# Sums of squares stored as rows, the last results of a projection stored at once, and four more weight blocks split ahead, in a two-attention encoder layer

## The chip, the cores and the metric

The kernel runs on one core of a Trainium2 chip. A core has TensorE (PE; its weight loads are listed as PEld), VectorE (DVE), ScalarE (ACT), GpSimd (POOL) and SyncE (SP), which here only issues DMAs; 16 DMA engines move data between HBM and the core's own memory. The metric is the device time of one execution in microseconds: the median of three runs, and beside it one profiled execution, whose trace gives every instruction's start and length.

## The reference

One encoder layer is applied to two independent requests of 2048 tokens each (a "prompt" and a "sample") with the same weights, in float32:

```
h    = RMSNorm(x)                                  # x: 2048 x 1024
proj = h @ w_in    -> q_a 512 | k_a 128 | v_a 128 | g_a 512 | q_b 512 | k_b 512 | v_b 512 | g_b 512
o_a  = windowed GQA (8 query heads, 2 key heads, +-128 tokens, QK-norm, partial rotary, sink) * SiLU(g_a)
o_b  = 2-D neighbourhood attention (8 heads, grid 32 x 64, QK-norm, position bias)            * SiLU(g_b)
x    = x + concat(o_a, o_b) @ w_out                # 1024 x 1024
y    = x + (p @ w_ple) * sigmoid(x @ w_ple_gate)   # p: 2048 x 256
```

## The kernel before, in words

**Precision by splitting.** TensorE multiplies in a reduced float32 format, so each operand is split into a high part (a rounded copy) and a low part (the rest), and each product is made of three: high x high, high x low, low x high. A weight block is 128 x 512; split it is 128 x 2 x 512 (512 KB). Splitting takes one ScalarE instruction for the high part and one VectorE instruction for the low one.

**Fillers and units.** The work is written as two streams that are woven together. *Fillers* are the projections of one tile of 128 tokens: `proj_a(f)` for f = 0 to 31 (attention A, 16 tiles per request), then `proj_b(f)` for f = 32 to 95 (attention B, whose heads are done in two halves of four: f = 32 to 63, then 64 to 95). *Units* are the attention of one tile. A table of fractions (PLAN_A, PLAN_B) says at which point of a filler each step of a unit is issued; attention lags its projection by 2 tiles in A and by 6 in B. The order on TensorE is fixed by hand (every matmul is pinned behind the one before). For the other engines and for the DMA queue a planner orders the instructions at build time by the order in which they are written and by its own estimate of when each is ready; `P(...)` pins an instruction behind the one written just before it on the same engine, and `behind(...)` pins one behind the last matmul.

**Weights of attention B split ahead.** While A's 28 fillers f = 2 to 29 run, `presplit` takes one weight block each: it loads the raw block (256 KB) into a staging buffer of tag `raw`, splits it in the middle of the filler, and at the next filler stores both parts to HBM (`parts_d`, 512 KB). It handles 28 of the 32 blocks of attention B; the other four (second half, `wb`, odd j) are copied as they are to HBM (`plain_d`). When the stream reaches a half, `load_w` loads its 16 blocks: `wa` while the last two tiles' second projections run, `wb` after them. A whole block in parts is one load; a plain one is loaded raw and its split is put on a list (`jobs`) that the fillers work off.

**Sums for the last stage.** `combine` forms sums and differences of the quarters of `w_out` and `w_ple_gate` in 8 rounds of six steps: load 1 MB into the same `raw` buffer, four subtractions or additions on POOL, store 1 MB. Each `proj_b` from f = 32 on takes one step, every eighth takes two; all is done at f = 75. From then on `presplit` handles 16 more blocks (of `w_ple` and `w_out`), one per tile.

**The norm.** In A each tile's mean square (`ms`, one number per token, so one column of 128 x 1) is made from a second, token-major load of x (`stn<-x_n`, two of 256 KB per tile) by two ScalarE squares. B's tiles hold the tokens in another order, so every `proj_a` stores its column to HBM (`ms_d`, L601), and at the end of each request `regroup` lists 16 gathers (`ms_b<-ms_d`, L639) that bring the numbers back in B's order, two per filler.

**The last layers' results.** When the fillers run out, the stream turns to `ple_ahead(n)`, n = 0 to 7, which makes p @ w_ple for 512 tokens in 8 blocks of six matmuls; each block goes from PSUM (tag `pj`, three banks) by a ScalarE copy to a buffer `ev` and by DMA to HBM (`ple_d`). The store is written one step late: `store_ple(1)` issues the store of the block before. The first five n run beside the last attention units; the last three are the tail: TensorE has nothing else to do, `ev` rotates through five buffers of tag `s`, and between them the first loads of the last stage are written (`load_raw`, 1 MB each; `load_x`, 256 KB each; `load_q`, four of 256 KB).

**The last stage** multiplies by `w_out` and `w_ple_gate` with seven block products in place of eight (`product`, accumulators `acca` and `accc`). Its first product puts its four column blocks into PSUM tags `ms`, `ms`, `pj`, `pj`.

Of the kernel before, what the change touches and what calls it, by code (L numbers as in the profile page):

```python
# [11 lines left out]
F32 = mybir.dt.float32  # L12
# [5 lines left out]
SEQ = 2048  # L18
DM = 1024
NT = SEQ // 128  # L20
# [80 lines left out]
def emit(ctx, tc, io):  # L101
# [73 lines left out]
    def w_block(half, tag, j):  # L175

        if half == "p":
            return io["w_ple"][128 * j:128 * j + 128, 512 * tag:512 * tag + 512]
        if half == "o":
            h, c = int(tag[2]) - 1, int(tag[1]) - 1  # L180
            return io["w_out"][512 * h + 128 * j:512 * h + 128 * j + 128, 512 * c:512 * c + 512]
        c0 = 1280 + 1024 * half + (512 if tag == "wb" else 0)
        return io["w_in"][128 * j:128 * j + 128, c0:c0 + 512]

    def load_w(half, tag):

        ws = []
        hold[0], step[0] = HOLD[tag], 4
        for j in range(KT):
            w = main.tile([128, 2, 512], F32R, tag=f"{tag}{j}", name=f"{tag}{j}", bufs=1)  # L190
            if (half, tag, j) in parts_d:
                nc.sync.dma_start(w.bitcast(F32), parts_d[half, tag, j])
            else:
                raw = w[:, 1].bitcast(F32)
                nc.sync.dma_start(raw, plain_d[half, tag, j])
                jobs.append((f"{tag}{j}", partial(split_w, w, raw, nw[:, j:j + 1], P)))
            ws.append(w)
        return ws

# [2 lines left out]
    def presplit(load):  # L202

        if load:
            if due:
                key, t, slot = due.pop()
                nc.sync.dma_start(parts_d[key], t[:, 0:2].bitcast(F32))
            if to_split:
                if not pre:
                    pre.extend([ap.tile([128, 4, 512], F32R, tag="raw", name="pre", bufs=1), 0])  # L210
                pre[1] += 1
                due.append((to_split.pop(0), pre[0], 2 + pre[1] % 2))
                key, t, slot = due[0]
                nc.sync.dma_start(t[:, slot].bitcast(F32), w_block(*key))
        elif due:
            key, t, slot = due[0]
            raw, sc = t[:, slot].bitcast(F32), nw[:, key[2]:key[2] + 1]
            if key[0] in ("p", "o"):
                behind(nc.scalar.copy(t[:, 0], raw))
                behind(nc.vector.tensor_tensor(out=t[:, 1], in0=raw, in1=t[:, 0].bitcast(F32), op=ALU.subtract))  # L220
            else:
                behind(nc.scalar.activation(t[:, 0], raw, AF.Copy, scale=sc))
                behind(nc.vector.scalar_tensor_tensor(out=t[:, 1], in0=raw, scalar=sc, in1=t[:, 0].bitcast(F32),
                                                      op0=ALU.mult, op1=ALU.subtract))
# [192 lines left out]
    for i in range(2):  # L417
        split(1, i)
    blocks = [(half, tag, j) for half in range(2) for tag in ("wa", "wb") for j in range(KT)]
    parts_d = {(half, tag, j): dram.tile([128, 2, 512], F32, tag=f"sp_{half}{tag}{j}", name=f"sp_{half}{tag}{j}")  # L420
               for half, tag, j in blocks if half == 0 or tag == "wa" or j % 2 == 0}
    for half, tag, j in [("p", m, j) for m in range(2) for j in range(2)] + \
            [("o", name, j) for name in ("a11", "a12", "a22") for j in range(4)]:
        parts_d[half, tag, j] = dram.tile([128, 2, 512], F32, tag=f"sp_{half}{tag}{j}", name=f"sp_{half}{tag}{j}")
    to_split = list(parts_d)
    plain_d = {}
    for key in blocks:
        if key not in parts_d:
            plain_d[key] = dram.tile([128, 512], F32, tag="pl_%d%s%d" % key, name="pl_%d%s%d" % key)
            copies.append((plain_d[key], w_block(*key)))  # L430
    sums = [dram.tile([4, 128, 4, 512], F32, tag=f"sums{i}", name=f"sums{i}") for i in range(2)]
    w_gate_c = copied(io["w_gate"], DM, 1024)
    snk = ap.tile([128, 2, 8], F32, tag="snk", name="snk")
# [58 lines left out]
    def proj_a(f):  # L492
# [105 lines left out]
        else:  # L598
            gate()
        held[f] = q, gs, y  # L600
        P(nc.sync.dma_start(ms_d[128 * f:128 * f + 128].rearrange("(p c) -> p c", c=1), ms))  # L601
        if t == NT - 1:
            regroup(s)
        else:
            regroup_next()
# [155 lines left out]
    def proj_b(f):  # L761
        half, st = divmod(f - 2 * NT, 2 * NT)
        s, j = divmod(st, NT)
        b, cb = divmod(j, 4)
        if f < 2 * NT + 8:
            regroup_next()
        if not ks_b:
            ks_b.extend(big([128, 32, 2, 64], F32R, f"ks_b{e}") for e in range(2))
        w_qk, w_vg = w_b[half]
        xr = xt.pop(f)  # L770
        pk = ptile([128, 512], "pj", "pqk")
        for i, c in enumerate(project(pk, xr, lambda k, b: ready("wa", k, w_qk)[:, b, :], 215)):
            at = i + 24 if f in last else i
            if i == PD and f == 2 * NT + 9:
                stats_b(1)
            if at in HX:
                split(f + 1, HX[at])
            if i == PA and combined and (to_split or due):
                presplit(True)
            yield c  # L780
        sq = ap.tile([128, 512], F32, tag="sq", name="sqb", bufs=2)
        nc.scalar.activation(sq, pk, AF.Square)
        ssq = ap.tile([128, 8], F32, tag="ssq", name="ssqb", bufs=3)
        nc.vector.tensor_reduce(out=ssq, in_=sq.rearrange("p (h d) -> p h d", d=HD), op=ALU.add, axis=AX.X)
        vr = ap.tile([128, 8], F32, tag="vr", name="vrb", bufs=2)
        y = ap.tile([128, 8], F32, tag="y", name="yb", bufs=4)
        nc.vector.tensor_scalar(out=vr, in0=ssq, scalar1=1.0 / HD, scalar2=ep_b[:, st:st + 1],  # L787
                                op0=ALU.mult, op1=ALU.add)
        rsqrt(vr, y, 8)
        qg = ap.tile([128, 2, 4, HD], F32, tag="qg", name="qg", bufs=6)  # L790
        kt = ap.tile([128, 4, HD], F32, tag="kt", name="kb", bufs=2)
        def normed():

            for dst, c in ((kt, 4), (qg[:, 0], 0)):
                behind(nc.vector.tensor_tensor(out=dst, in0=pk[:, 64 * c:64 * c + 256].rearrange("p (h d) -> p h d", d=HD),
                                               in1=y[:, c:c + 4].unsqueeze(2).broadcast_to([128, 4, HD]), op=ALU.mult))
        yield 0, False
        pv = ptile([128, 512], "pj", "pvg")
        for i, c in enumerate(project(pv, xr, lambda k, b: ready("wb", k, w_vg)[:, b, :], 215)):
            if i + 24 in HX and f not in last:  # L800
                split(f + 1, HX[i + 24])
            if i == (PR if f not in last else 1):
                normed()
            if i == PA + 16:
                presplit(False)
            yield c
            if i == (KB if f not in last else 10):
                if f < 2 * NT + 2:
                    pending.append((kt, b, cb))
                else:  # L810
                    keys_b(kt, b, cb)
        v = ap.tile([128, 4, 2, HD], F32R, tag="sq", name="vb", bufs=2)
        vp = pv[:, 0:256].rearrange("p (h d) -> p h d", d=HD)
        nc.scalar.activation(v[:, :, 0, :], vp, AF.Copy, scale=rs_b[:, st:st + 1])
        nc.vector.scalar_tensor_tensor(out=v[:, :, 1, :], in0=vp, scalar=rs_b[:, st:st + 1],
                                       in1=v[:, :, 0, :].bitcast(F32), op0=ALU.mult, op1=ALU.subtract)
        for w, (c0, ncol) in COL_WIN.items():
            lo, hi = max(c0, 16 * cb), min(c0 + ncol, 16 * cb + 16)
            if lo < hi:
                nc.sync.dma_start(v_d[half, s, w][8 * b:8 * b + 8, lo - c0:hi - c0].rearrange("r c h a d -> c r (h a d)"),  # L820
                                  v[8 * (lo - 16 * cb):8 * (hi - 16 * cb)].bitcast(F32).rearrange("p h a d -> p (h a d)"))
        gs = qg[:, 1].rearrange("p h d -> p (h d)")
        nc.scalar.activation(gs, pv[:, 256:512], AF.Tanh, scale=hr_b[:, st:st + 1])
        nc.vector.scalar_tensor_tensor(out=gs, in0=gs, scalar=1.0, in1=pv[:, 256:512], op0=ALU.add, op1=ALU.mult)
        held[f] = qg[:, 0], gs
        for _ in range(2 if f % 8 == 4 else 1):
            if next(combining, 0) == 0:
                combined.append(f)
        yield 0, False
# [152 lines left out]
    def store_ple(n):  # L982

        for dst, ev in made[:n]:
            nc.sync.dma_start(dst, ev)
        del made[:n]

    def ple_ahead(n, tail=False):

        load_p(n + 1)  # L990
        for m in range(KT):
# [14 lines left out]
                ev = ap.tile([128, TW], F32, tag=("ev", "sq")[m // 2 % 2], name="ev", bufs=3 - m // 2 % 2)  # L1006
            P(nc.scalar.copy(ev, ps))
            store_ple(1)
            made.append((ple_d[n][:, m], ev))

    qs = {}

# [98 lines left out]
                keys_b(*p)  # L1111
            owed = 16
    drain(stream)
    store_ple(1)


    ab_stack.close()
    with tc.tile_pool(name="c", bufs=1, reuse_waits="tile") as op:
# [183 lines left out]
            piece(0, k)  # L1302
        load_q(0, "s2")
        drain(rest)
        store_ple(1)
        for _ in range(4):
            load_x()
        for name in ("s1", "s3", "s4"):
# [95 lines left out]
```

## Time and profile before

| | |
|---|---|
| median of 3 runs | 2491.75 us (2488.02 to 2493.52) |
| the profiled execution | 2489.69 us, its span 2487.9 us |
| fillers of A with A's attention | 0 to about 720 us |
| turn to B's first half, then fillers 34 to 37 alone | about 720 to 812 us |
| first half of B, second half of B | about 812 to 1191, 1245 to 1740 us, the turn between them |
| p @ w_ple beside the last units, then alone | about 1740 to 1831 to 1871 us |
| last stage | 1871 us to the end |
| DMA | 438.87 MB, mean 176 GB/s |

How to read it: a row of a wait names who stood idle and what came last before it went on; a row of the chain gives a start, a length and the work; a row of SyncE's queue gives an issue of a DMA and not its landing. "PEclk" or the column before the DMA share is the clock that TensorE was granted, 1.00 being full speed.

### The profile page before, as it was taken

The page shows a single profiled execution, that of the slowest core. Times are in us where ns is not written, and L with a number is a line of the kernel's source. Part 1 is how long each engine was busy: PE and PEld are TensorE (multiplying, and loading weights), DVE is VectorE, ACT ScalarE, POOL GpSimd, SP SyncE. Part 2 cuts the span into 40 slices and gives each one's busy share as a digit, 9 for nine tenths or more (in the row PEclk, how much of TensorE's full clock was granted, in tenths as well). Part 3 has the DMA queues.
Part 4 walks back from the last instruction along what each step waited for, and adds up shares of the span by engine and source line. Part 5 has one row for each costly group of instructions (what it writes and reads, how often), then busy time and mean ns, then how long its engine had stood idle before and what let it go on. Part 6 is the DMA issues. An engine that isn't in the chain of part 4 may idle for free.

```text
span 2487.9 us, 40537 instructions
## 1 busy us (share of the span) xinstructions
PE 2459.3 (99%) x13048; PEld 2078.0 (84%) x13048; DVE 1702.9 (68%) x4210; ACT 1413.9 (57%) x3405; POOL 863.4 (35%) x1365
## 2 busy tenths in 40 slices
PE   9999999999999999999999999999999999999999
PEld 7888888888878888888788888888777888888887
DVE  6777777777765666666666666666536655687776
ACT  6777776777664665565656566666653222344443
POOL 5555555555444544544444444443100000000000
PEclk9999999999999999999999999999999999999999
DMA  7655554455374566555855566667876445756765
GB/s 204 143 111 96 98 88 102 96 92 98 82 195 137 167 190 183 169 167 184 288 171 184 177 205 210 199 198 239 295 255 233 161 169 175 267 171 219 243 227 169
DMA packets 247140, 438.87 MB, mean 176 GB/s; under 512 B 32400, under 2 KB 86800, under 8 KB 241680
## 3 DMA queue, kind: packets, MB, share of 16 engines
q1 hardware_dynamic: 246640, 436.27, 59.6%
q8 instruction: 104, 1.70, 0.3%
q14 instruction: 108, 0.88, 0.1%
q10 hardware_dynamic: 288, 0.01, 0.0%
HBM read 308.24 MB, written 133.19 MB: 177 GB/s over the span
## 4 chain that ended last, share of the span: by engine, by line
PE 91%; DMA 4%; DVE 3%; ACT 1%; issue 1%; POOL 0%; SPq 0%; ACTq 0%; DVEq 0%; POOLq 0%
PE pqk L255 14%; PE acca L1226 14%; PE pvg L255 14%; PE accc L1226 10%; PE pg L255 6%; PE pq L255 5%; PE scb L255 4%; PE ptb L258 3%; PE pob L255 3%; PE pple L255 3%; PE pk L255 3%; PE po L255 3%; PE sc L255 3%; PE pt L258 2%; DMA stn<-x_n 1%; DMA vw<-v_d 1%
## 5 line engine op out<-in xcount | busy, mean ns | idle before, releaser
L287 ACT ACTIVATE s<-s,nm 128x320 f32<-128x320 f32 (+6 forms) x512 | 294.4, 576 | 314.9 <-DVE nm L282 193.9
L255 PE MATMUL pvg<-wb,xr 128*128 128x512 f32 x1536 | 462.6, 408 | 1.3 <-DMA wb<-sp_0wb 0.6
L255 PE MATMUL pqk<-wa,xr 128*128 128x512 f32 x1536 | 442.9, 410 | 0.0
L255 PEld LDWEIGHTS pqk<-wa,xr 128*128 128x128 f32 x1536 | 266.1, 189 | 36.9
L255 PEld LDWEIGHTS pvg<-wb,xr 128*128 128x128 f32 x1536 | 266.7, 189 | 34.2 <-DMA wb<-sp_0wb 2.2
L1208 ACT CAST opd<-raw 128x512 fp32r<-128x512 f32 x224 | 131.5, 618 | 273.3 <-PE acca L1226 115.2
L356 POOL TENSOR_TENSOR xr<-stx,xr 128x512 fp32r<-128x512 f32 x188 | 241.6, 1295 | 106.3 <-ACT xr L355 84.0
L1209 DVE TENSOR_TENSOR opd<-raw,opd 128x512 fp32r<-128x512 f32 x224 | 146.4, 685 | 151.7 <-ACT opd L1208 151.7
L255 PE MATMUL pg<-wb,xr 128*128 128x512 f32 x768 | 233.5, 410 | 1.8 <-DVE vv L518 1.0
L255 PE MATMUL pq<-wa,xr 128*128 128x512 f32 x768 | 219.4, 400 | 0.0
L271 DVE CUSTOM_DVE_ANT_0 s<-scb,bias 128x288 f32<-128x288 f32 (+3 forms) x256 | 142.0, 555 | 104.6 <-PE scb L255 104.5
L137 POOL TENSOR_TENSOR yb<-vrb,power 128x8 f32<-128x8 f32 x64 | 106.5, 1664 | 236.1 <-DVE vrb L787 222.6
L1226 PE MATMUL accc<-opd,wb 128*128 128x512 f32 x768 | 176.7, 389 | 0.0
L1226 PE MATMUL acca<-opd,wa 128*128 128x512 f32 x768 | 176.6, 391 | 0.0
L1226 PE MATMUL acca<-opd,s 128*128 128x512 f32 x768 | 175.4, 389 | 0.0
L1226 PEld LDWEIGHTS acca<-opd,wa 128*128 128x128 f32 x768 | 145.1, 189 | 30.3
L1226 PEld LDWEIGHTS accc<-opd,wb 128*128 128x128 f32 x768 | 144.2, 188 | 29.9
L1226 PEld LDWEIGHTS acca<-opd,s 128*128 128x128 f32 x768 | 144.2, 188 | 29.9
L918 DVE TENSOR_TENSOR otb<-pob,otb 64x512 f32<-64x512 f32 x128 | 88.1, 689 | 112.8 <-ACT otb L917 111.2
L255 PEld LDWEIGHTS pob<-p_t,vw 128*128 128x128 f32 (+2 forms) x832 | 133.0, 189 | 27.6 <-DVE p_t L899 5.0
L255 PEld LDWEIGHTS pq<-wa,xr 128*128 128x128 f32 x768 | 135.1, 189 | 17.3
L715 DVE TENSOR_TENSOR pr<-pt,pr 128x512 fp32r<-128x512 f32 (+2 forms) x248 | 135.5, 549 | 16.5 <-ACT pr L713 13.2
(167 smaller groups left out, 5177.0 us busy)
## 6 DMA issues: line engine op xcount, KB each, us to landing
stx<-x_b SPq DMA_DIRECT2D x128, 256.0 KB
vw<-v_d SPq DMA_DIRECT2D x112, 256.0 KB
stx<-x_a SPq DMA_DIRECT2D x64, 256.0 KB
stn<-x_n SPq DMA_DIRECT2D x64, 256.0 KB
v_d<-vb SPq DMA_DIRECT2D x64, 256.0 KB
ple_d<-ev SPq DMA_DIRECT2D x64, 256.0 KB
xres<-x_r SPq DMA_DIRECT2D x64, 256.0 KB
x_d<-r SPq DMA_DIRECT2D x64, 256.0 KB
```

Source lines behind the costliest of these rows:

```text
L137: nc.gpsimd.tensor_tensor(out=y, in0=v, in1=power.broadcast_to([128, n]), op=ALU.pow)
L255: pinned(nc.tensor.matmul(out, lhsT, rhs, start=start, stop=stop))
L258: pinned(nc.tensor.transpose(out, in_, eye))
L271: nc.vector.tensor_tensor_reduce(out=s, in0=ps[:, :n], in1=bias, scale=1.0, scalar=-3.0e38, op0=ALU.add, op1=ALU.max, accum_out=sm["mx"][: ...
L287: ex = nc.scalar.activation(ss[i], ss[i], AF.Exp, bias=nm[:, i:i + 1], accum_out=den[:, i:i + 1])
L356: low.tensor_tensor(out=lo, in0=raw, in1=hi.bitcast(F32), op=ALU.subtract)
L715: nc.vector.tensor_tensor(out=pr[r, 1, to], in0=pt[r, c], in1=pr[r, 0, to].bitcast(F32), op=ALU.subtract)
L918: nc.vector.tensor_tensor(out=ot[a:a + 64], in0=pq[a:a + 64], in1=ot[a:a + 64], op=ALU.add)
L1208: P(nc.scalar.copy(hi, v))
L1209: P(nc.vector.tensor_tensor(out=lo, in0=v, in1=hi.bitcast(F32), op=ALU.subtract))
L1226: pinned(nc.tensor.matmul(ps, w[k][:, a, c:c + 128], o[:, b], start=i in (0, 1, 4) and k == 0 and j == 0, stop=k == 3 and j == 2, skip_gro ...
```

## The change

1. `proj_a` no longer stores its column of mean squares. At the last tile of each request the 16 columns are transposed by TensorE into a PSUM buffer of tag `ms`, copied by ScalarE into a buffer of tag `sq`, and stored as 16 rows of 128 numbers (512 B) in one DMA.
2. In the tail, `ple_ahead` writes each store right behind its own copy; the step that was owed at the end is dropped in both places.
3. All 32 blocks of attention B are split ahead. The list of raw copies in HBM and the split at the load are gone. The 28 fillers of A still take 28 blocks; the last four (second half, `wb`, j = 4 to 7) are taken by f = 34 to 37, stored by f = 38, and the staging buffer is then given free.
4. `combine` starts at f = 39 and takes two steps at every third tile, one at the others; it is done at f = 75.

```diff
@@ load_w
-            if (half, tag, j) in parts_d:
-                nc.sync.dma_start(w.bitcast(F32), parts_d[half, tag, j])
-            else:
-                raw = w[:, 1].bitcast(F32)
-                nc.sync.dma_start(raw, plain_d[half, tag, j])
-                jobs.append((f"{tag}{j}", partial(split_w, w, raw, nw[:, j:j + 1], P)))
+            nc.sync.dma_start(w.bitcast(F32), parts_d[half, tag, j])
@@ presplit
-            if to_split:
+            if to_split and (to_split[0][0] in (0, 1) or combined):
                 if not pre:
                     pre.extend([ap.tile([128, 4, 512], F32R, tag="raw", name="pre", bufs=1), 0])
...
                 nc.sync.dma_start(t[:, slot].bitcast(F32), w_block(*key))
+            else:
+                pre.clear()
@@ emit
-               for half, tag, j in blocks if half == 0 or tag == "wa" or j % 2 == 0}
+               for half, tag, j in blocks }
...
-    plain_d = {}
-    for key in blocks:
-        if key not in parts_d:
-            plain_d[key] = dram.tile([128, 512], F32, tag="pl_%d%s%d" % key, name="pl_%d%s%d" % key)
-            copies.append((plain_d[key], w_block(*key)))
@@ proj_a
-        P(nc.sync.dma_start(ms_d[128 * f:128 * f + 128].rearrange("(p c) -> p c", c=1), ms))
         if t == NT - 1:
+            ps = ptile([128, 512], "ms", "pms")
+            tr(ps[:NT, :128], ms_a[:, NT * s:NT * s + NT])
+            row = ap.tile([128, 512], F32, tag="sq", name="row", bufs=2)
+            P(nc.scalar.copy(row[:NT, :128], ps[:NT, :128]))
+            P(nc.sync.dma_start(ms_d[s * SEQ:(s + 1) * SEQ].rearrange("(t p) -> t p", p=128), row[:NT, :128]))
             regroup(s)
@@ proj_b
-            if i == PA and combined and (to_split or due):
+            if i == PA and f >= 2 * NT + 2 and (to_split or due):
                 presplit(True)
...
-        for _ in range(2 if f % 8 == 4 else 1):
+        for _ in range(0 if f < 2 * NT + 7 else 2 if f % 3 == 0 else 1):
             if next(combining, 0) == 0:
                 combined.append(f)
@@ ple_ahead
             store_ple(1)
-            made.append((ple_d[n][:, m], ev))
+            if tail:
+                nc.sync.dma_start(ple_d[n][:, m], ev)
+            else:
+                made.append((ple_d[n][:, m], ev))
@@ after drain(stream), and after drain(rest)
-    store_ple(1)
```

More of the change, by code (lines that the diff above doesn't have):

```diff
@@ L1304, in emit @@
         drain(rest)
-        store_ple(1)
         for _ in range(4):
```

## The prediction

> **What bounds the kernel now.** I read the page first (its engine totals and the shares of the chain that ended last), then the trace cut into stages, then the list of TensorE's own waits, and last the chain and SyncE's queue around the longest of them.
>
> ```profile
> span 2487.9 us, 40537 instructions
> PE 2459.3 (99%) x13048; PEld 2078.0 (84%) x13048; DVE 1702.9 (68%) x4210; ACT 1413.9 (57%) x3405; POOL 863.4 (35%) x1365
> PE 91%; DMA 4%; DVE 3%; ACT 1%; issue 1%; POOL 0%; SPq 0%; ACTq 0%; DVEq 0%; POOLq 0%
> ```
>
> TensorE is busy 99% of the span and makes 91% of the chain. No matmul is added or taken away here (two tiny transposes apart), so a gain can only come out of the places where TensorE stands still or runs slowly. The stages (the columns are time, then busy time of PE, PEld, DVE, ACT, POOL, the granted clock, DMA share, GB/s) say where those are:
>
> ```profile
> 0.00:720.00 720.00, 709.09 (x4247) 620.22 (x4248) 546.21 (x1679) 505.06 (x1396) 382.31 (x793) 1.00 0.54 114
> 1191.00:1245.00 54.00, 52.55 (x281) 42.81 (x280) 36.61 (x88) 34.16 (x77) 23.15 (x26) 1.00 0.86 294
> 1245.00:1740.00 495.00, 495.00 (x2700) 416.29 (x2698) 334.16 (x849) 306.17 (x723) 217.51 (x252) 1.00 0.63 197
> 1740.00:1831.00 91.00, 87.77 (x480) 73.11 (x479) 51.04 (x130) 64.28 (x151) 13.88 (x28) 0.98 0.79 270
> 1831.00:1871.50 40.50, 34.82 (x149) 28.19 (x148) 7.71 (x13) 17.44 (x32) 0.73 (x1) 0.94 0.90 306
> 1871.50:2488.00 616.50, 610.57 (x2688) 504.92 (x2687) 424.49 (x678) 211.55 (x377) 0.00 (x0) 1.00 0.61 201
> ```
>
> And the waits of TensorE itself (who it waited for: us in total, times, longest):
>
> ```profile
> PE pple L255 <- ACT ev L1007: 5.7, 1, 5.7
> PE pt L258 <- DVE ot L742: 5.4, 2, 4.9
> PE pob L255 <- DMA vw<-v_d: 2.6, 4, 1.5
> PE pg L255 <- DVE vv L518: 1.0, 1, 1.0
> PE pktb L258 <- DVE kb L795: 0.7, 1, 0.7
> PE pvg L255 <- ACT wb L151: 0.4, 1, 0.4
> PE pvg L255 <- DVE wb L152: 0.3, 1, 0.3
> ```
>
> Two single waits, of 5.7 and 4.9 us, are most of it. Each part of the change touches one group of these waits, so I take them in that order.
>
> **Part 1, the sums of squares.** The wait of 4.9 us lies at 679.35. The chain there (start, length, what), SyncE's queue, and ScalarE's wait in it:
>
> ```profile
> 666.34 9.18 DMA stn<-x_n
> 675.60 0.69 ACT stn L369 x2
> 678.89 0.42 DVE ot L742
> 679.35 1.12 PE pt L258 x4
> ```
>
> ```profile
> 662.75 0.80 SPq L601 DMA_DIRECT2D ms_d<-ms_a  x1
> 666.34 1.58 SPq L338 DMA_DIRECT2D stn<-x_n  x2
> ```
>
> ```profile
> ACT stn L369 <- DMA stn<-x_n: 4.9, 1, 4.9
> ```
>
> ScalarE's square stands in its queue in front of the attention's output copies, and it waits for a 256 KB load that needs 9.18 us. Why so long? An undisturbed load of the same kind takes a third of that, and during the slow one the DMA engines are half busy but move almost nothing (second fence, first row; its other two rows are used below):
>
> ```profile
> 35.04 2.83 DMA stn<-x_n
> ```
>
> ```profile
> 667.00:674.00 7.00, 7.00 (x43) 6.00 (x42) 2.84 (x13) 2.39 (x9) 4.58 (x13) 1.00 0.50 20
> 679.40:682.00 2.60, 2.60 (x13) 2.60 (x14) 2.48 (x6) 1.67 (x4) 0.00 (x0) 0.50 0.18 53
> 1868.60:1873.00 4.40, 4.40 (x11) 3.43 (x12) 0.00 (x0) 1.37 (x4) 0.00 (x0) 0.50 1.03 393
> ```
>
> A share of 0.50 at 20 GB/s means packets that sit and wait. What went out just ahead is the store of one column of `ms_a`, 128 separate words of 4 bytes side by side in one 512-byte stretch of HBM. My reading is that those 128 small writes hold up the load behind them. The Trainium skill (DMA: Bandwidth & Descriptors, Specifications) states that a transfer under 512 B is done as a read-modify-write; the row of 20 GB/s agrees, though the page does not say that others are held up.
>
> The change takes all 32 of these stores out and puts two in, each of 16 rows of 512 B. At 666.34 the load should then need about 2.8 us and be there near 669.2 (the second of the pair, 1.2 us later, near 670.5), while ScalarE is busy with exponentials until about 675.60 - 4.9 = 670.7. So 4.9 us of idle time go. After the wait TensorE runs 2.6 us at a granted clock of 0.50, which costs 2.6 / 2 = 1.3 us. In the stretch from 1191 to 1245, whose waits are 0.7 us at most, the clock is 1.00 throughout, so I let the half clock go with the wait. **Gain 6.2 us.** The Trainium skill (TensorE: Matmul & The Clock Gate, Part 1) puts the half rate down to an idle window of about 3.4 us; the trace agrees, since the 0.50 stands behind waits of 4.9 and 5.7 us, and by that rule a wait that is only halved would already give back the same 1.3 us. What is late next is nothing that I can see: VectorE itself waited for ScalarE there. The other 30 column stores cost TensorE nothing that the list of waits shows, since the loads behind them had time; 32 issues of up to 0.8 us leave SyncE's queue, where nothing was late because of them. The 32 gathers of the same words (`ms_b`) stay.
>
> Added at tiles 15 and 31: one transpose, one PSUM buffer of tag `ms`, one copy, one 8 KB store.
>
> ```profile
> L258 PE MATMUL pt<-ident,s 128*128 128x128 f32 x616 | 98.4, 273 | 6.1 <-DVE ot L742 5.4 <-DVE den L295 0.7
> L741 DVE TENSOR_TENSOR ot<-po,ot 64x256 f32<-64x256 f32 x128 | 54.0, 422 | 89.9 <-ACT ot L738 89.0
> ```
>
> A transpose is at most 0.27 us. It must wait for one of two `ms` buffers, which the output copies give back; VectorE's part of that sat idle 89.9 / 128 = 0.7 us before each, two of them per buffer. Bounds: 0.1 us (pipelined) to 0.27 + 1.4 + 0.8 = 2.5 us each. I take 0.25 each, near the lower end, since the plan issues the buffer's last copies ahead of it (`fin` at 0.45 of a half unit of 720 / 64 = 11.2 us, the new transpose near 0.59, so 1.5 us). **Cost 0.5 us.** The queue behind the store (weight loads for the next stage) waits for one copy of about 0.6 us.
>
> **Part 2, results stored at once.** SyncE's queue and the chain at the longest wait:
>
> ```profile
> 1853.29 3.30 SPq L1245 DMA_DIRECT2D xres<-x_r  x4
> 1856.64 0.43 SPq L1158 DMA_DIRECT2D raw<-oa_d  x1
> 1857.12 0.50 SPq L1160 DMA_DIRECT2D raw<-ob_d  x1
> 1857.72 2.05 SPq L985 DMA_DIRECT2D ple_d<-ev  x3
> ```
>
> ```profile
> 1857.72 10.09 DMA ple_d<-ev
> 1868.55 2.93 PE pple L255 x6
> ```
>
> The 24 last copies rotate through five buffers of tag `s`. Counted from 0, copy 20 reuses the buffer of copy 15. The store of copy 15 is written one step late, so it stands behind four loads of 256 KB and two of 1 MB, 3 MB in all, and lands after 10.09 us. TensorE's last six products need the PSUM bank that copy 20 frees. With the store written at its own copy, `load_x` and both `load_raw` are pinned behind it; it goes out in their place, about 1854, with nothing large ahead, and lands some 3 us later. Copy 20 is due near 1861: the wait began at 1868.55 - 5.7 = 1862.9, and its products ended two blocks of six earlier, 2.7 us before that. Copy 21 now waits, for the store of copy 16, which stays behind the 3 MB. But the last products need only copies up to 20, and the first two column blocks of the next product use `ms` banks. Only the third uses a bank that copy 21 frees. It begins 24 products later. At the last stage's rate (610.57 / 2688 = 0.227 us) TensorE would end the last six near 1864.2 and those 24 near 1869.7. The stores behind the 3 MB landed at 1857.72 + 10.09 = 1867.8, so the margin is 1.9 us. So the 5.7 us go, and with them the half clock of the quoted 4.4 us, 2.2 us. **Gain 7.9 us.** Moving the store puts the six loads behind it some 0.7 us later, which the margin takes. If it doesn't, the third block waits for what is missing.
>
> **Part 3, the last four blocks.** At the turn to the second half, four of eight `wb` blocks are loaded raw and split on the spot, and the splits sit in ScalarE's and VectorE's queues until the load is there:
>
> ```profile
> 1225.82 7.17 DMA wb<-pl_1wb
> 1233.01 0.73 ACT wb L151
> 1233.76 0.75 DVE wb L152
> ```
>
> They account for 0.4 + 0.3 us of TensorE's waits and, as the chain runs on from them through VectorE to `kb`, for the 0.7 us of `pktb`. **Gain 1.4 us.** Against it stand 4 x 256 KB = 1 MB more to load. At the stage's 294 GB/s that is 3.5 us of queue, the upper bound of a cost.
>
> ```profile
> 1223.30 0.58 SPq L623 DMA_DIRECT2D sums<-raw  x1
> ```
>
> But this 1 MB store now leaves the stage. Counting steps (two at every third tile from 39), stores fall at tiles 60 and 65, none at 63. Bytes balance, so I take 0. The four raw copies in HBM go too, and the eight copies of `w_gate` behind them move up by two tiles, to tiles 2 to 5; no wait of TensorE above is laid to them, 0. The same four splits return at tiles 34 to 37, where projections run alone, each about 0.73 + 0.75 us in two engines that are not the bound. Their 4 x 768 KB there meet a combining that no longer runs before tile 39.
>
> The combining keeps its 32 operations on POOL and ends at tile 75 as before. New is that at tiles 39, 48, 57 and 66 the first operation follows its own load at once, so POOL may stand until 1 MB is there.
>
> ```profile
> L137 POOL TENSOR_TENSOR yb<-vrb,power 128x8 f32<-128x8 f32 x55 | 91.6, 1665 | 218.0 <-DVE vrb L787 204.5 <-DMA stx<-x_b 9.0 <-DMA raw<-w_gate 4.4
> ```
>
> POOL idles 218.0 / 55 = 4.0 us ahead of each of these anyway. Bounds for the four: nothing, if the load takes the 2.83 us of an undisturbed one; 10.09 - 4.0 = 6.1 us each, if it is as slow as the slowest quoted. I take 0: DMA is not full outside the turns. Behind a standing POOL are the gate products and `o_tb`, for which VectorE waits.
>
> **Sum**, against the profiled execution's own 2489.69 us (span 2487.9): -6.2 + 0.5 - 7.9 - 1.4 = -15.0, so 2474.7. The median of the runs shown stands 2.1 us above that execution; from 2491.75 it is **2476.8**.
>
> **Rivals.**
>
> *The slow loads are slow by themselves* (reading `x_n`, not the stores). For: the first stage, the only one that reads `x_n`, moves 114 GB/s at a DMA share of 0.54, the second half of B 197 at 0.63, so slow packets are common in it. Against: the 2.83 us at 35.04, the same load with no such store just ahead. Then only parts 2 and 3 count: -7.9 - 1.4 + 0.5 = -8.8, 2483.0.
>
> *The tail's wait comes back elsewhere*, on copy 21, on the 1 MB loads, or because copy 15 itself comes late and the pinned loads wait with it. For: DMA runs at 0.90 there and the margin is 1.9 us. Against: the loads' total stays the same. Then -6.2 - 1.4 + 0.5 = -7.1, 2484.7.
>
> *Slower*: POOL stands behind the sums' loads at the four tiles, VectorE waits for `o_tb` and TensorE for VectorE. At 6.1 us each plus the half clock after it (1.3 to 2.2, say 1.7) that is 31 us, less 15 gained: 2508. It decides from 15 / 4 = 3.8 us per place. Against it: between 1245 and 1740 TensorE waits for nobody.
>
> **How the numbers follow.** 0.2% (5 us) is about what a measurement of this kernel can tell from no change. The sum above 0.60; slow loads by themselves 0.10; tail not mended 0.10; both failing, or a reshuffled order eating the gain, 0.09 (about 2490); slower 0.11. The first three are faster by over 0.2%: 0.80. The likeliest case alone: 2471 to 2481, its low end taking in the 1.0 us of `vv`, 2.5 us of `vw` and the spread of the runs, its high end 2 us per transpose. The range reaches to the two partial cases and a little beyond: 2470 to 2487.
>
> **What would show it.** Part 1: no `ms_d` issue but two, `stn` landing in about 3 us throughout, no wait of `pt` near 679, no half clock there. Part 2: the store ahead of `xres`, `pple` waiting for nothing, `acca` starting some 14 us earlier than 1871.5 (6.2 - 0.5 + 1.4, then 5.7 and half of 2.9 at the half clock). Part 3: no `wb` split. Wrong would be: slow `stn` with `ms_d` gone; a new wait at `acca`'s third block; POOL idle over 5 us on `raw`.

## The result, and the profile after

| | before | after |
|---|---|---|
| median of 6 runs | 2492.64 us (2488.02 to 2497.40) | 2473.18 us (2471.06 to 2475.98) |
| the profiled execution | 2489.69 us, span 2487.9 | 2471.06 us, span 2469.3 |

The ratio is 0.9922, 95% interval 0.9908 to 0.9935: faster by 19.5 us between the medians and by 18.6 us between the two profiled executions, where 15.0 was forecast. The time lies inside the forecast range, 3.6 us below its number.

The page of the kernel after, its span, engine totals and shares of the chain:

```profile
span 2469.3 us, 40518 instructions
PE 2453.0 (99%) x13050; PEld 2074.3 (84%) x13050; DVE 1703.7 (69%) x4210; ACT 1413.2 (57%) x3407; POOL 861.5 (35%) x1365
PE 93%; DVE 3%; DMA 2%; ACT 1%; issue 1%; POOL 0%; SPq 0%; ACTq 0%; DVEq 0%; POOLq 0%
```

The DMA share of the chain fell from 4% to 2%; the engines do what they did. The stages, with the tail cut at its new end (columns as before: time, busy time of PE, PEld, DVE, ACT, POOL, granted clock, DMA share, GB/s). The times are the same as for the kernel before, but the kernel after runs some microseconds ahead and so holds slightly later work in each of them:

```profile
1191.00:1245.00 54.00, 54.00 (x296) 45.29 (x295) 34.10 (x87) 32.88 (x75) 26.40 (x29) 1.00 0.87 301
1245.00:1740.00 495.00, 495.00 (x2697) 415.93 (x2696) 336.91 (x849) 308.39 (x727) 215.56 (x251) 1.00 0.64 201
1740.00:1831.00 91.00, 88.47 (x484) 73.59 (x483) 47.30 (x122) 63.59 (x148) 14.57 (x29) 1.00 0.80 272
1831.00:1853.80 22.80, 22.80 (x102) 18.88 (x101) 4.10 (x7) 11.56 (x21) 0.00 (x0) 1.00 0.97 327
1853.80:2469.00 615.20, 609.76 (x2689) 504.39 (x2687) 425.35 (x680) 212.64 (x379) 0.00 (x0) 1.00 0.61 206
```

TensorE has no gap left in the turn to the second half (54.00 of 54.00) and none in the tail (22.80 of 22.80). What it still waits for:

```profile
PE pob L252 <- DMA vw<-v_d: 1.8, 4, 0.7
...
PE pg L252 <- DVE vv L510: 1.0, 1, 1.0
...
PE pqt L255 <- ACT row L597: 0.5, 1, 0.5
PE pms L255 <- DVE ot L737: 0.5, 1, 0.5
```

The two long waits, 5.7 us for `ev` and 4.9 us for `ot`, are gone, and so are those for `wb` and `kb` at the turn. New are the two of 0.5 us that belong to the transposes.

**Where the time went, place by place.** The order of the matmuls is the same in both kernels, apart from the two transposes. So one can take the start of the same weight load in both traces and see how far the kernel after leads. The lead changes only at a few places, and the stretches left out add less than 0.1 us each (times are those of before):

```
place (us)                      forecast   lead gained in the profiled executions
0-58     the start                 0        -0.5
58-65    third tile                0        +0.8
345-355  transpose of tile 15     -0.25     -0.8
676-700  the wait of 4.9 us        6.2      +5.2
700-720  transpose of tile 31     -0.25     -0.9
720-768  turn to the first half    0        +1.9
768-1191                           0        -0.3
1191-1245 turn to the second half  1.4      +2.5
1245-1740 second half              0         0.0
1740-1780 last attention units     0        +2.3
1780-1862                          0         0.0
1862-1875 the tail                 7.9      +8.2
1875-end                           0         0.0
sum                               15.0      18.4 (18.5 read at the end)
```

**Part 1.** The stretch ahead of the old wait and the one in which it lay, first in the kernel before, then after:

```profile
661.00:668.00 7.00, 7.00 (x53) 6.68 (x52) 6.85 (x23) 4.67 (x10) 5.13 (x9) 1.00 0.50 101
668.00:680.00 12.00, 7.12 (x41) 6.01 (x40) 4.06 (x15) 6.66 (x21) 3.65 (x12) 0.95 0.38 85
```

```profile
661.00:668.00 7.00, 7.00 (x54) 6.73 (x53) 6.84 (x23) 5.14 (x11) 4.73 (x8) 1.00 0.27 99
668.00:680.00 12.00, 11.38 (x74) 9.99 (x72) 9.11 (x31) 7.63 (x23) 5.71 (x14) 1.00 0.44 141
```

In the 12 us from 668 on, TensorE stands still for 0.6 us instead of 4.9, at a clock of 1.00 instead of 0.95, and DMA moves 141 GB/s at a share of 0.44 instead of 85 at 0.38. In the seven microseconds that the prediction quotes, 667 to 674, it had moved 20 GB/s at a share of 0.50; now it moves 194 at 0.61. The effect is not local to that wait. Between 60 and 660 us, first before, then after:

```profile
60.00:660.00 600.00, 599.36 (x3645) 527.35 (x3646) 466.31 (x1452) 428.84 (x1207) 323.30 (x681) 1.00 0.52 102
```

```profile
60.00:660.00 600.00, 598.99 (x3644) 526.65 (x3643) 465.47 (x1449) 427.10 (x1205) 322.40 (x680) 1.00 0.31 98
```

About the same bytes per second need a DMA share of 0.31 instead of 0.52.

**Part 2.** SyncE's queue in the tail, and TensorE's products there:

```profile
1842.43 1.68 SPq L1006 DMA_DIRECT2D ple_d<-ev  x2
1844.20 1.83 SPq L1243 DMA_DIRECT2D xres<-x_r  x4
...
1847.39 1.58 SPq L1006 DMA_DIRECT2D ple_d<-ev  x3
```

```profile
1834.77 19.20 PE L252 MATMUL pple<-p_r,wa 128*128 128x512 f32 x84
1853.81 11.04 PE L1224 MATMUL acca<-opd,wa 128*128 128x512 f32 x48
```

The store of copy 15 is the second of the two in the first row. It goes out at 1843.79, ahead of the loads at 1844.20, and has landed at 1846.21. The products run through without a gap and `acca` begins at 1853.81, 17.5 us earlier than before (1871.28). ScalarE still waits in that stretch (us in total, times, longest):

```profile
ACT ev L1003 <- DMA ple_d<-ev: 7.3, 3, 6.0
```

The 6.0 us are copy 21, which waits for a store behind the 3 MB, as foreseen. TensorE does not notice.

### The profile page after: what moved, and what is told of

It is laid out like the page before. It is cut to its first block, busy times and chain, and to the rows that moved or that the text cites. A ratio compares the mean times of both kernels' runs of the same rounds, so it can differ in the third digit from the quotient of the medians.

```text
span 2469.3 us, 40518 instructions
## 1 busy us (share of the span) xinstructions
PE 2453.0 (99%) x13050; PEld 2074.3 (84%) x13050; DVE 1703.7 (69%) x4210; ACT 1413.2 (57%) x3407; POOL 861.5 (35%) x1365
## 4 chain that ended last, share of the span: by engine, by line
PE 93%; DVE 3%; DMA 2%; ACT 1%; issue 1%; POOL 0%; SPq 0%; ACTq 0%; DVEq 0%; POOLq 0%
PE pvg L252 14%; PE acca L1224 14%; PE pqk L252 14%; PE accc L1224 10%; PE pq L252 6%; PE pg L252 6%; PE scb L252 4%; PE ptb L255 3%; PE pob L252 3%; PE pple L252 3%; PE po L252 3%; PE pk L252 3%; PE sc L252 3%; PE pt L255 2%; DVE pr L711 1%; DMA vw<-v_d 1%
```

## The experiments

All times are compared with the kernel before on the same chip. "Lead" is the comparison of starts used above.

### Each part alone

**Part 1 alone** in the kernel before:

```diff
-        P(nc.sync.dma_start(ms_d[128 * f:128 * f + 128].rearrange("(p c) -> p c", c=1), ms))
         if t == NT - 1:
+            ps = ptile([128, 512], "ms", "pms")
+            tr(ps[:NT, :128], ms_a[:, NT * s:NT * s + NT])
...
```

> The kernel before with part 1 alone (row stores of the mean squares in place of the column stores). If the column stores hold up the loads behind them: the median landing of the x_n loads falls from 7.9 us to about 2.8, TensorE's wait near 679 goes, TensorE gains 5 us there and 1 to 2 us at the turn near 721 to 760, less about 1 us at the two transposes; in all -5 to -7 us, about 2486.5. If the x_n loads are slow by themselves: landing stays near 8 us and the time stays at 2492.

Measured: 2482.39 us against 2492.87, ratio 0.9960 (0.9945 to 0.9975), so -10.5 us. The tail's wait stays, as it must:

```profile
PE pple L255 <- ACT ev L1011: 4.6, 1, 4.6
```

In its profiled execution the lead over before grows by 0.8 at 60, 4.4 at 679 and 1.6 between 720 and 768, and falls by 0.8 and 0.9 at the two transposes. That is part 1's pattern in the kernel after, the gain at the first turn included. The rest of this execution's lead of 7.6 us lies at places that part 1 does not touch: 1.6 us between 1740 and 1780, and 1.4 in the tail, whose wait happened to be 4.6 us instead of 5.7.

**Part 2 alone:**

```diff
-            made.append((ple_d[n][:, m], ev))
+            if tail:
+                nc.sync.dma_start(ple_d[n][:, m], ev)
+            else:
+                made.append((ple_d[n][:, m], ev))
...
-    store_ple(1)
...
-        store_ple(1)
```

> The kernel before with part 2 alone (tail stores at their own copy). If the store of copy 15 behind 3 MB of loads is the cause, TensorE loses its wait of 5.7 us near 1868 and the half clock after it: -8 us, about 2484.5, with the trace up to 1831 as before, the wait near 679 and the half clock near 1774 included. If the gain needs the other parts, less than 4 us.

Measured: 2485.80 us, ratio 0.9971 (0.9961 to 0.9981), -7.1 us. The lead grows by 8.25 us between 1862 and 1875. In this execution `accc` gives 1.2 us of it back right behind; in the full change nothing is given back, and why no run shows.

**Part 3 alone**, made from the kernel after by undoing parts 1 and 2:

```diff
+        P(nc.sync.dma_start(ms_d[128 * f:128 * f + 128].rearrange("(p c) -> p c", c=1), ms))
         if t == NT - 1:
-            ps = ptile([128, 512], "ms", "pms")
...
-            if tail:
-                nc.sync.dma_start(ple_d[n][:, m], ev)
-            else:
-                made.append((ple_d[n][:, m], ev))
+            made.append((ple_d[n][:, m], ev))
...
```

> The kernel before with part 3 alone (all blocks split ahead, combining from tile 39). If the splits at the load cost what the trace of before shows: TensorE gains 1.4 to 2.5 us near 1234 and nothing else, 2490. If the gain of 2.2 us that the changed kernel has between 1756 and 1778 comes from this part, it shows here too (2488) and the half clock near 1774 is gone; if it comes from the column stores or is chance, it isn't there.

Measured: 2491.89 us, ratio 0.9997 (0.9988 to 1.0006), -1.0 us and not to be told from no change. Between 1191 and 1245 the lead does grow by 1.6 us. So it does in every trace with part 3: by 0.9 to 2.5 us over before in all nine, and by 0.1 to 0.5 in the three without it. Both long waits are there, each longer than in the profiled execution of before:

```profile
PE pt L255 <- DVE ot L734: 6.5, 2, 5.5
PE pple L252 <- ACT ev L999: 6.3, 1, 6.3
```

The three alone add up to 10.5 + 7.1 + 1.0 = 18.6 us against 19.5 together: the parts act each at its own place.

**One store of part 2.** If only the store of copy 15 counts, a single early `store_ple` ahead of the loads must give all of it:

```diff
         drain(ple_ahead(AHEAD + 1, True))
+        store_ple(1)
         for _ in range(4):
```

> The kernel before with one call added: the one store that is owed when the seventh block row of the tail ends (that of copy 15) is issued ahead of the four loads of 256 KB and the two of 1 MB. If that store alone is the cause: the same -8 us as with all tail stores moved, 2484.5. If the others matter as well, less than half of it.

Measured: 2485.84 us, ratio 0.9976 (0.9966 to 0.9986), -7.0 us, the same as for all stores of the tail; the lead grows by 8.25 us at the same place, and 2.0 us go again by 1900. So it is this one store.

### What makes the column stores dear

Part 1 takes away 32 stores and adds two, and it could help because there are fewer small writes, because fewer issues stand in SyncE's queue, or because 128 words no longer lie side by side. These runs separate that. The first writes the same 32 columns into spare memory, word beside word; the second writes them 512 B apart. In both, nobody reads the words: they are extra stores beside the kernel's own work.

```diff
+    spare_d = dram.tile([2 * SEQ], F32, tag="spare_d", name="spare_d")
...
+        P(nc.sync.dma_start(spare_d[128 * f:128 * f + 128].rearrange("(p c) -> p c", c=1), ms))
         if t == NT - 1:
```

> The changed kernel with its 32 column stores put back, to a spare place in HBM that nobody reads: 128 words of 4 bytes side by side per store. If these stores hold up the loads behind them: the x_n loads need about 8 us again, TensorE waits about 5 us near 677, and the time is 5 to 7 us above the changed kernel's 2473. If not: 2473.

```diff
+    spare_d = [dram.tile([128, 128], F32, tag=f"spare_d{f}", name=f"spare_d{f}") for f in range(2 * NT)]
...
+        P(nc.sync.dma_start(spare_d[f][:, 0:1], ms))
         if t == NT - 1:
```

> As the one with the column stores put back, but each word goes to a row of its own, 512 bytes apart, still 128 words of 4 bytes per store. If it is the words' lying side by side (many small writes to one short stretch of HBM) that makes them slow: the x_n loads stay near 2.8 us and the time at 2473. If every small write is slow in itself, wherever it goes: as slow as side by side, 5 to 7 us above.

Measured: side by side 2484.30 us (ratio 0.9969, 0.9958 to 0.9981), 11.1 us above the kernel after; 512 B apart 2473.42 us (0.9929, 0.9912 to 0.9946), the same as the kernel after. Number, size and issue of the stores and their place in the queue are equal in the two. The 600 us of the first stage, side by side and then apart:

```profile
60.00:660.00 600.00, 597.68 (x3632) 524.65 (x3632) 466.62 (x1451) 428.22 (x1200) 321.84 (x677) 1.00 0.53 99
```

```profile
60.00:660.00 600.00, 599.02 (x3643) 526.57 (x3642) 465.38 (x1448) 427.15 (x1205) 322.48 (x680) 1.00 0.31 98
```

The share goes back to 0.53 with the words side by side and stays at 0.31 with the same words apart. With the share the wait comes back: TensorE's longest one side by side, and the load on the chain there.

```profile
PE pt L256 <- DVE ot L740: 7.3, 3, 5.1
```

```profile
670.98 8.87 DMA stn<-x_n
```

How far apart they must be was asked with 64 and 256 B, again with spare stores that nobody reads, and one execution of each:

```diff
+    spare_d = [dram.tile([128, 16], F32, tag=f"spare_d{f}", name=f"spare_d{f}") for f in range(2 * NT)]
...
+        P(nc.sync.dma_start(spare_d[f][:, 0:1], ms))
```

> As the spare column stores with the words 512 bytes apart, but 64 bytes apart. If the unit that small writes to the same place contend for is 64 bytes or less: x_n loads near 2.8 us, about 2473. If it is larger: between 2.8 and 8.4 us and a longer wait near 677.

With `[128, 64]` in place of `[128, 16]`:

> The same, 256 bytes apart. Unit of 256 bytes or less: x_n loads near 2.8 us, about 2473. If 512 bytes are needed: in between.

Measured: 2474.67 and 2473.79 us. The load on the chain of the run with 64 B, at the place of the old wait (it is 4.35 us with part 1 alone, too):

```profile
667.74 4.35 DMA stn<-x_n
```

From each DMA's issue to the last of its landing signals in the trace, the medians between 60 and 660 us:

```
                                    before  after  side by side  64 B   256 B  512 B apart
the column's store (512 B in all)     9.38    -        9.85      2.77   2.42   2.49
stn<-x_n (256 KB)                     7.87   2.81      8.37      2.80   2.77   2.76
pre<-w_in (256 KB)                    8.73   3.38      8.90      3.06   2.98   3.15
```

A spacing of 64 B is already enough; between 4 and 64 B nothing was tried. The loads that suffer are those issued while a column's store is on its way: the `stx` loads of the same stretch, issued some 12 us or more behind it, land after a median of 2.8 us in before as in after. The Trainium skill (DMA: Bandwidth & Descriptors, Specifications), which the prediction weighed at this place, puts a transfer under 512 B down to a read-modify-write. All these words fall under that, and those 64 B apart or more are not slow. So by these runs it is not the size of the write that costs but the neighbour. What happens inside the memory or the DMA engine no run shows.

**Columns apart, and used.** Then the transposes should not be needed either:

```diff
-    ms_d = dram.tile([2 * SEQ], F32, tag="ms_d", name="ms_d")
+    ms_d = dram.tile([2 * SEQ, 128], F32, tag="ms_d", name="ms_d")
...
+        P(nc.sync.dma_start(ms_d[128 * f:128 * f + 128, 0:1], ms))
         if t == NT - 1:
-            ps = ptile([128, 512], "ms", "pms")
-            tr(ps[:NT, :128], ms_a[:, NT * s:NT * s + NT])
-            row = ap.tile([128, 512], F32, tag="sq", name="row", bufs=2)
-            P(nc.scalar.copy(row[:NT, :128], ps[:NT, :128]))
...
-        rows = ms_d.rearrange("(r k c) -> r k c", k=4, c=16)
+        rows = ms_d[:, 0].rearrange("(r k c) -> r k c", k=4, c=16)
```

> The changed kernel without the transposes: every tile stores its column of mean squares again, but each word 512 bytes from the next, and the gathers read them from there. If only the words' lying side by side was slow: x_n loads near 2.8 us, gathers no slower than in the changed kernel, no wait at 350 and 710 for PSUM, and 1 us less than the changed kernel's 2473: 2472. If gathers of words 512 bytes apart are slow: above 2475, with waits at the turn near 710 to 760.

Measured: 2472.34 us, ratio 0.9924 (0.9911 to 0.9938). It saves 0.7 us at 350 and 0.8 us at 710, the places of the transposes, and is still not to be told from the kernel after: leads of 1 us come and go elsewhere from execution to execution.

**The transposes in other banks.** Their cost was put at 0.25 us each, with a wait for an `ms` buffer as the upper bound. They take a `pj` buffer here:

```diff
-            ps = ptile([128, 512], "ms", "pms")
+            ps = ptile([128, 512], "pj", "pms")
```

> The changed kernel with the two transposes of the mean squares in a PSUM bank of tag pj (three banks) in place of ms (two). If the wait for an ms bank is what the transposes cost: TensorE's waits of 0.5 us on pms and 0.5 us on pqt behind ACT row go, 0.5 to 1.3 us gained at 350 and 710, too little for the time (2472.5). If a pj bank is as late, it waits there in the same measure.

Measured: 2471.79 us, ratio 0.9918 (0.9904 to 0.9933), again not to be told from the kernel after. The lead over it grows by 0.7 us at 350 and again at 710, as much as without any transpose, so nearly all that the transposes cost is the wait for the `ms` buffers; it is lost again at 676 and soon after 710.

### The bytes at the turn

Part 3 loads 1 MB more at the turn and no longer stores 1 MB there; the cost was taken as 0 with 3.5 us as the bound. A copy of 1 MB within HBM, of no other use, was written ahead of the eight loads of `wb`:

```diff
         hold[0], step[0] = HOLD[tag], 4
+        if (half, tag) == (1, "wb"):
+            for i in range(2):
+                nc.sync.dma_start(spare_d[i], parts_d[0, "wa", i])
```

> The changed kernel with 1 MB copied within HBM just ahead of the eight wb loads of the second half (an extra copy whose result is not used). If the turn's bytes were in balance with nothing to spare: TensorE waits 2.6 to 5 us for wb near 1225 to 1235. If there is room: no wait, 2473.

Measured: 2475.22 us, ratio 0.9930 (0.9915 to 0.9945), 2.0 us above the kernel after by the medians, inside the spread. But this run does not test the turn. Its edit leaves the copies unpinned, and in its trace SyncE's queue issues them in the first stage, some 1100 us ahead of it:

```profile
64.09 0.49 SPq L192 DMA_DIRECT2D spare_d<-sp_0wa  x1
...
85.52 0.49 SPq L192 DMA_DIRECT2D spare_d<-sp_0wa  x1
```

So at the turn it moves the same bytes as the kernel after. All the same it falls behind it by 1.6 us between 1191 and 1245, and TensorE waits for `wb` there:

```profile
PE pvg L256 <- DMA wb<-sp_1wb: 0.4, 1, 0.4
```

The kernel with the transposes in other banks, which has no byte more there either, falls behind by 1.0 us in the same stretch, with a wait of the same kind:

```profile
PE pvg L252 <- DMA wb<-sp_1wb: 0.3, 1, 0.3
```

These differences come with the execution, and what an extra MB costs at the turn no run shows. The turn has little room left: where the same work lies in the kernel after, from 1185 to 1239, the DMA share is 0.95 at 327 GB/s, and its loads come just in time, or a little late.

## Why the prediction was right or wrong

**Right in sign, place and mechanism.** The column stores held up the loads, the store of copy 15 held up the tail, and the splits held up the turn. The first two are shown by runs in which each alone was taken away, the first also by putting it back. The third is too small for the time: it shows in the leads at the turn and in the waits that are gone there. The gain was underestimated, and the time came out 3.6 us lower than forecast. By the steps:

- *Part 1, the wait at 679: 6.2 forecast, 5.2 in the profiled executions.* The wait of 4.9 us went. Of the 1.3 us for the half clock the lead shows little: it grows by 1.3 us during the slow matmuls and falls again by 1.2 us within the next microsecond, where other engines set the pace. At half speed TensorE had lost time that it would have lost anyway.
- *"The other 30 column stores cost TensorE nothing that the list of waits shows": the step that failed.* At the turn to the first half, two stores of columns went out between the loads of `wb` and `stx`. SyncE's queue of the kernel before, and the chain there:

```profile
702.87 0.46 SPq L601 DMA_DIRECT2D ms_d<-ms_a  x1
703.71 0.32 SPq L192 DMA_DIRECT2D wb<-sp_0wb  x1
705.80 1.59 SPq L338 DMA_DIRECT2D stx<-x_b  x2
707.43 0.42 SPq L601 DMA_DIRECT2D ms_d<-ms_a  x1
707.95 8.51 SPq L192 DMA_DIRECT2D wb<-sp_0wb  x7
```

```profile
705.80 9.60 DMA stx<-x_b
715.46 13.05 DMA wb<-sp_0wb
```

  The pair of 256 KB loads took 9.60 us on the chain and a load of 512 KB 13.05. In the kernel after the same pair lands after 2.7 and 3.2 us and the eight loads of `wb` after 3.2 to 7.9. The prediction looked for column stores only behind the two long waits. TensorE's explicit waits for those blocks are short, but its weight loads wait too. From the view of the tile `wb` in before, 700 to 780 us:

```profile
who waited for it (us, times):
...
  PEld pvg L255: 2.2, 5
...
  PE pvg L255: 0.6, 2
```

  The lead grows by 1.9 us there. When the stores come back side by side, the same stretch from 720 to 768 loses 3.6 us. The 0.8 us at 60 is less sure: of the five traces with adjacent columns two have it as well (part 2 alone and the single store), while all eight without them do.
- *Part 1 as a whole is worth more than one profile shows.* Its places add up to 0.8 - 0.8 + 5.2 - 0.9 + 1.9 = 6.2 us in the profiled pair, but alone it measured -10.5, and putting back the stores, with the transposes kept, measured +11.1. The profiled execution of before was a mild one, 3.0 us under the median of six: its longest wait near 679 was 4.9 us, against 5.1, 5.5, 5.8 and 6.8 in the four other kernels with adjacent columns, whose half clock there lasts 6.83 us instead of 3.41. A stall set by such loads varies, and the sum was made from one sample of it. The leads of all the traces bear this out. At 770 us, where the column stores are past, the four others with adjacent columns are 2.2 to 7.1 us behind before, and the eight without them 4.5 to 6.3 us ahead of it. Between the means of the two groups lie 9.7 us, near the 10.5 and 11.1 of the medians; the forecast's 5.7 for part 1, less the transposes, came from the mildest of the five.
- *The transposes: 0.5 forecast, 1.6 measured* (0.8 and 0.9), inside the bounds. The buffer wait that was thought to be hidden is there: 0.5 us for `pms` at tile 15, and at tile 31 0.5 us at a later user of the `ms` buffers, `pqt`, which waits for ScalarE to copy the row. That second wait was not in the working.
- *Part 2: 7.9 forecast, 8.2 measured* at the place, and 7.1 between medians. The margin at `acca`'s third block held, and one store alone does it. The "copy 21 waits" that the rival built on happened (6.0 us) without effect.
- *Part 3: 1.4 forecast, 2.5 measured in the full change, 1.6 alone.* The waits named are gone. That the bytes cost nothing was argued from their balance, and no run tests it.
- *From 1740 to 1780: 0 forecast, 2.3 in the profiled pair.* These are the waits for `vw` and a half clock of 3.41 us behind them. Before, then after:

```profile
1764.00:1784.00 20.00, 18.10 (x93) 14.76 (x92) 8.67 (x25) 11.76 (x29) 2.45 (x5) 0.91 0.86 295
```

```profile
1764.00:1784.00 20.00, 19.16 (x104) 15.97 (x105) 10.10 (x28) 13.02 (x31) 2.44 (x5) 1.00 0.88 289
```

  TensorE stands still 1.1 us less and the clock is 1.00 instead of 0.91. (The work of the first row lies 8 to 10 us earlier in the kernel after; there, too, the clock is 1.00.) This belongs to no part of the change: the half clock is there in before, in part 2 alone, in the single store, and in the runs with 1 MB copied and with columns 64 and 256 B apart; it is absent in the other kernels, part 3 alone and the columns side by side among them. It seems to come and go with the execution; whether the changes shift its odds stays open.

**The rivals.** *Slow loads by themselves* fell: a 256 KB load takes 2.81 us with the stores gone and 8.37 with them back. *The tail's wait elsewhere* fell. *Slower, by POOL*, fell in an instructive way. POOL did stand behind the sums' loads (POOL's waits in the kernel after, between 812 and 1740 us):

```profile
POOL raw L617 <- DMA raw<-w_out: 8.3, 2, 4.3
...
POOL raw L617 <- DMA raw<-w_gate: 3.7, 1, 3.7
```

These are three waits, of 4.3 us at 834.97, 4.0 at 982.02 and 3.7 at 1273.26, about the 3.8 us from which the rival was to decide. But the lead changes by 0.3 us from 768 to 1191 and not at all from 1245 to 1740. What hung behind POOL had more slack than the 4.0 us that POOL's own idle time showed; the rival's price for TensorE was wrong.

## What to carry to other kernels

Do not store one number per partition side by side into HBM while other transfers matter: make rows of it first, or put the words 64 B apart. In the list of waits look for a cause at every place where it can act, weight loads and other loads' durations included, and not only behind the longest wait; and when a stall comes from a slow transfer, one profiled execution is one sample of it. Where a tail rotates through few buffers, what frees the next buffer goes out ahead of large prefetches, even if they are needed soon. And where a planner orders the queue, look in the trace for the place at which an added transfer really went out before reading anything from its time.

## What the runs showed of the hardware that was not expected

- A store of 128 words of 4 bytes, side by side in 512 B of HBM, lands after 9.4 to 9.9 us; the same words 64, 256 or 512 B apart land after 2.8, 2.4 and 2.5 us.
- While it is under way, loads of 256 KB of quite other data, issued on the same queue, need a median of 7.9 to 8.9 us instead of 2.8 to 3.4, and the DMA engines show a share of 0.52 instead of 0.31 for the same rate of about 100 GB/s.
- In the middle of these runs the half clock comes in spells of 3.41, 6.83 and 10.24 us, one, two or three times the same length, mostly behind waits of about 5 us, but at 1774 of the kernel before also behind waits of which the longest is 1.5 us. The Trainium skill (TensorE: Matmul & The Clock Gate, Part 1) names a free-running window of about 3.4 us for it; the trace agrees in these lengths. It does not follow that a spell costs half its length: at 679 the net was some 0.1 us for 2.6 us at 0.50, while in the tail, where TensorE alone sets the pace, the lead grew by 2.2 us over the 4.4 us at 0.50.
